# Gate and up weights fetched half a pair ahead, in one ring of eight tiles shared with the down projection

## The chip, the cores and the metric

The kernel runs on one core of a Trainium2 chip. The metric is the device time of one execution in microseconds; the time before is the median of three runs, 2311.24 us (2308.6 to 2313.23). All data are float32, and products are made on TensorE from operands that are split into a high and a low part.

## The reference

One decoder layer over 2048 tokens and 16 meta tokens, model width 1024, feed-forward width 2816. What matters here is the end of the layer:

```python
h = layer_norm(ALPHA * h + mix, ln1_g[l], ln1_b[l])          # mix: attention and gated linear attention, projected
ffn = swiglu(h, w_ffn_gate[l], w_ffn_up[l], w_ffn_down[l])   # silu(h @ w_gate) * (h @ w_up), then @ w_down
h = layer_norm(ALPHA * h + ffn, ln2_g[l], ln2_b[l])
return h[:, N_META:]
```

## The kernel before

The layer runs in stages. Up to about 920 us: input norm, projections, window attention, the chunked gated linear attention, and the output projection, tile by tile. Then gate and up (about 937 to 1858 us), then the down projection (1858 to 2292 us) with the last norm. The end of the output projection overlaps the first products of gate and up, in an order written out by hand (`FIRST_PRODUCTS`).

**Gate and up.** The tokens are in two blocks `tb` of 1024, the feed-forward width in `NP` = 11 pairs `p` of two tiles of 128. For each `(tb, p)` the product of a 2x2 blocked weight with a 2x2 blocked activation is made by a Strassen scheme: seven products instead of eight, in the order b11, t2, t1, b21, t3, t4, b22. `weights(p, tb)` allocates the four weight quarters `a11, a21, a22, a12` (128x1024 float32, 512 KB each) in the ring with the tag `x2` and four tiles, issues their loads on SP (L1307), and then yields, product by product, the split factor: GpSimd makes `s1 = a21 + a22` (L1319), then `a21 = a11 - a21`, `a11 = s1 - a11` and `a12 = a12 - a11` in place (L1315). `parts` copies a quarter rounded (ScalarE, L183) and takes the rest (L184: GpSimd for pa11, ps2, pa12, pa22, VectorE for ps1, ps3, ps4) into one of four tiles `whl`. The trace names the quarters `a`, their factors `pa` and `ps`. TensorE makes 24 matmuls of 128x512 for each product (L195: `b` and `t`), into two banks. VectorE adds products together (L1382: `u`, `c`, `p`), gates them (L1332, L1333: `sa`, `sb`), GpSimd combines the results (L1414 to L1420: `sc`, `s`), and SP stores seven pieces of each pair to DRAM (L1361).

The activation operands `h_b...`, `h_t...` of a block are split once per block (`make`: loads at L670 and L673 into a ring `mk` of three, L183/L184 on ScalarE, VectorE and GpSimd) and stay in SBUF. Those of the second block are made inside the last pair of the first (about 1400 to 1470 us). Their sums are made by `combine` (L632 to L638, `cb`), which the code puts in pairs 2 to 5 of the first block.

**Down projection.** Again seven products, in the order 1, 6, 7, 4, 5, 2, 3 (`MULS`), each over 11 tiles of the contraction in six steps (`GROUPS`: one tile, then five times two). A step of two tiles has 48 matmuls (L1196, `d`). `fetch_step(k)` loads the two activation tiles `rA` (L1166, or L1169) into a ring of four in the pool `dp`, and the weights into the ring `x2` (`quarter_of` at L1110, `kept` at L1116): one tile for products 1, 2, 3 and 5, two for 7 and 4, three for 6. GpSimd subtracts (L1101), product 6 keeps two results in DRAM (`keep`, L1121), and `split_step` makes the factors `A` and `B` (L183 on ScalarE, L184 on VectorE). A step is fetched two steps ahead and split one step ahead. At the end of each product VectorE takes the banks out (`end_product`, L1104 `y`), with residual rows loaded at L1231 and scaled by GpSimd at L1232.

**What sets the order.** The code only gives a program order and the tiles. The build is opened with `schedule_with_timeline_sim=True`: it simulates the program, and puts into each engine's queue, SP's included, what is ready in the simulation, earlier program order first. So a load or an addition can stand in its queue far ahead of its place in the code when its tile is free in the simulation. On the chip every queue runs strictly in that order. Pools opened with `reuse_waits="tile"` lie where closed pools lay, and a new tile there waits for the old ones under it.

Of the kernel before, what the change touches and what calls it, by code (L numbers as in the profile page):

```python
# [8 lines left out]
F32 = mybir.dt.float32  # L9
# [5 lines left out]
P = 128  # L15
D = 1024
# [4 lines left out]
NP = NF // 2  # L21
# [102 lines left out]
def body(ctx, tc, t, seq):  # L124
    nc = tc.nc
# [11 lines left out]
    NTB = seq // TF  # L137
# [44 lines left out]
    def split_into(hi, lo, src, lo_eng=None):  # L182
        nc.scalar.activation(hi, src, AF.Copy)  # L183
        (lo_eng or nc.vector).tensor_tensor(lo, src, r32(hi), op=ALU.subtract)  # L184
# [17 lines left out]
    def staging(name):  # L202
        return wpool.tile([P, D], F32, tag="x", name=name, bufs=3)
# [59 lines left out]
    with ExitStack() as c1:  # L263
# [5 lines left out]
        ps = c1.enter_context(tc.tile_pool(name="ps", bufs=1, space=PSUM))  # L269
# [350 lines left out]
    pools = {}  # L620
# [60 lines left out]
    ps = c1.enter_context(tc.tile_pool(name="gps", bufs=1, space=PSUM, reuse_waits="tile"))  # L681
# [394 lines left out]
    fp = hops.enter_context(tc.tile_pool(name="fp", bufs=1, reuse_waits="tile"))  # L1076
# [6 lines left out]
    def bank(name):  # L1083

        banks[0] += 1
        first = banks[0] <= 2 * len(EARLY) or (banks[0] - 1) % 8 < 4
        pool, tag = (psA, "a") if first else (pools["psB"], "b")
        return pool.tile([P, 512], F32, tag=tag, name=name, bufs=4)
# [11 lines left out]
    def sub(o, x, y):  # L1100
        nc.gpsimd.tensor_tensor(o, x, y, op=ALU.subtract)  # L1101
# [4 lines left out]
    def quarter_of(i, j, g, name):  # L1106

        ps = GROUPS[g]
        x = fp.tile([P, D], F32, tag="x2", name=f"w{i}{j}_{name}", bufs=4)[:, : 512 * len(ps)]
        nc.sync.dma_start(x.rearrange("p (a b) -> p a b", b=512), t["w_d"][i, j][:, ps[0] : ps[-1] + 1, :])  # L1110
        return x

    def kept(x, g, name):
        n = len(GROUPS[g])
        y = fp.tile([P, D], F32, tag="x2", name=f"{x}_{name}", bufs=4)[:, : 512 * n]
        nc.sync.dma_start(y.rearrange("p (a b) -> p a b", b=512), w_sc[x][g][:, :n, :])  # L1116
        return y

# [4 lines left out]
    def weights_of(q, g, name):  # L1123

        w = lambda i, j: quarter_of(i, j, g, name)
        if q == "1":
            return w(0, 0)
        if q == "6":
            w12, w11, w22 = w(0, 1), w(0, 0), w(1, 1)
            sub(w12, w12, w11)  # L1130
            keep("t1", g, w12)
            sub(w22, w22, w12)
            keep("s6", g, w22)
            return w22
        if q == "7":
            w22, w12 = w(1, 1), w(0, 1)
            sub(w22, w22, w12)
            return w22
        if q == "4":
            w21, s6 = w(1, 0), kept("s6", g, name)  # L1140
            sub(w21, w21, s6)
            return w21
        if q == "5":
            return kept("t1", g, name)
        return w(1, 0) if q == "2" else w(1, 1)
# [9 lines left out]
    raw, factors = {}, {}  # L1155

    def fetch_step(k):

        q, tbs, g = STEPS[k]
        nm = f"{q}_{tbs[0]}_{g}"  # L1160
        tile_ = lambda n: pools["dp"].tile([P, D], F32, tag="rA", name=f"rA{nm}_{n}", bufs=4)
        ps, xs = GROUPS[g], []
        if len(tbs) == NTB:
            for p in ps:
                xs.append(tile_(p)[:, : NTB * HT])
                nc.sync.dma_start(xs[-1].rearrange("p (a b) -> p a b", b=HT), a_sc[MULS.index(q)][p])  # L1166
        else:
            xs.append(tile_(ps[0])[:, : len(ps) * HT])
            nc.sync.dma_start(xs[0].rearrange("p (a b) -> p a b", b=HT), a_last[tbs[0]][:, ps[0] : ps[-1] + 1, :])  # L1169
        raw[k] = xs, weights_of(q, g, nm)  # L1170
# [128 lines left out]

    hops2 = ctx.enter_context(ExitStack())  # L1300
    c2 = ctx.enter_context(ExitStack())
    def weights(p, tb):
        nm = f"{tb}_{p}"
        raw = {}
        for a, (i, j) in (("a11", (0, 0)), ("a21", (1, 0)), ("a22", (1, 1)), ("a12", (0, 1))):
            raw[a] = fp.tile([P, D], F32, tag="x2", name=f"{a}_{nm}", bufs=4)
            nc.sync.dma_start(raw[a], t["w_gu"][p, i, j])  # L1307
        a11, a12, a21, a22 = (raw[a] for a in ("a11", "a12", "a21", "a22"))

        def parts(x, name, eng=None):  # L1310
            hl = wpool.tile([P, 2, D], F32R, tag="whl", name=f"{name}_{nm}", bufs=4)
            split_into(hl[:, 0, :], hl[:, 1, :], x, eng or nc.gpsimd)
            return hl

        sub = lambda o, x, y: nc.gpsimd.tensor_tensor(o, x, y, op=ALU.subtract)  # L1315
        s1 = fp.tile([P, D], F32, tag="s1", name=f"s1_{nm}", bufs=1)
        if (tb, p) != (0, 0) or not early:
            yield parts(a11, "pa11")
        nc.gpsimd.tensor_tensor(s1, a21, a22, op=ALU.add)  # L1319
        sub(a21, a11, a21)  # L1320
        sub(a11, s1, a11)
        yield parts(a11, "ps2")
        yield parts(s1, "ps1", nc.vector)
        yield parts(a12, "pa12")
        yield parts(a21, "ps3", nc.vector)
        sub(a12, a12, a11)
        yield parts(a22, "pa22")
        yield parts(a12, "ps4", nc.vector)
# [8 lines left out]
    AFTER, f = {}, None  # L1337
    for what in FIRST_PRODUCTS.split():
        if what[0] == "P":
            f = EARLY[int(what[1])]  # L1340
# [15 lines left out]
    for tb in range(NTB):  # L1356
        for p in range(NP):
            nm = f"{tb}_{p}"
            tl = lambda tag, n: [fp.tile([P, HT], F32, tag=tag, name=f"{n}{w}_{nm}", bufs=2) for w in range(2)]
            w = weights(p, tb)  # L1360
            store = lambda i, x: nc.sync.dma_start(a_last[tb][:, p, :] if i == 6 else a_sc[i][p][:, tb, :], x)  # L1361
            two = lambda x: staging(f"{x}_{nm}")[:, 0 : 2 * HT].rearrange("p (a q) -> p a q", q=HT)
            s4 = fp.tile([P, HT], F32, tag="s4", name=f"s4_{nm}", bufs=1)

            def product(f):
                if (tb, p) == (0, 0) and f in early:
                    banks[0] += 2
                    out = early[f]
                else:
                    hl, out = next(w), []  # L1370
                    for m in range(2):
                        out.append(bank(f"{f}{m}_{nm}"))
                        matmuls(out[m], ffn_terms(hl, ops[f], m))
                if p == NP - 1 and tb + 1 < NTB:
                    ops[f] = make(f, tb + 1)
                if (tb, p) == (0, 0) and f in AFTER:
                    finish_mixing(f)
                return out

            def add(o, x, y):  # L1380
                for i in range(2):
                    nc.vector.tensor_tensor(o[i], x[i], y[i], op=ALU.add)  # L1382

            p1, u2, u4 = tl("p1", "p1"), tl("u2", "u2"), tl("u4", "u4")
            for o, x in zip(p1, product("b11")):
                nc.scalar.activation(o, x, AF.Copy)
            add(u2, p1, product("t2"))
            add(u4, u2, product("t1"))
            add(p1, p1, product("b21"))
            if (tb, p) == (NTB - 1, NP - 1):  # L1390
                hops1.close()
                open_factors()
            sa = two("sa")
            c11 = gate(*p1, sa[:, 0])
            store(0, c11)
            p7 = product("t3")
            add(u2, u2, p7)
            c22 = tl("p1", "c22")
            add(c22, u4, p7)
            sb = two("sb")  # L1400
            c22 = gate(*c22, sb[:, 0])
            store(3, c22)
            add(u2, u2, product("t4"))
            c21 = gate(*u2, sb[:, 1])
            store(5, c21)
            add(u4, u4, product("b22"))
            if tb == 0 and NTB > 1 and 2 <= p < 2 + KT // 2:
                combine(1, p - 2, lambda n: pools["hop1"].tile([P, HT], F32, tag="mk", name=n, bufs=3))
            if (tb, p) == (NTB - 1, NP - 1):
                c2.close()  # L1410
                open_results()
            c12 = gate(*u4, sa[:, 1])
            sc = two("sc")
            nc.gpsimd.tensor_tensor(sc[:, 0], c12, c22, op=ALU.add)  # L1414
            store(4, sc[:, 0])
            nc.gpsimd.tensor_tensor(sc[:, 1], sc[:, 0], c11, op=ALU.subtract)
            store(1, sc[:, 1])
            nc.gpsimd.tensor_tensor(c12, c11, c12, op=ALU.subtract)
            store(2, c12)
            nc.gpsimd.tensor_tensor(s4, c21, sc[:, 1], op=ALU.subtract)  # L1420
            store(6, s4)
# [41 lines left out]
```

## Time and profile before

| | |
|---|---|
| median of 3 runs | 2311.24 us (2308.6 to 2313.23) |
| the profiled execution: its own time | 2313.99 us |
| its span, first to last instruction | 2312.2 us |
| TensorE (PE) busy | 2182.9 us, 94% |
| weight loads of TensorE (PEld) | 1872.3 us |
| VectorE (DVE) | 1583.1 us, 68% |
| GpSimd (POOL) | 1442.7 us, 62% |
| ScalarE (ACT) | 905.6 us, 39% |
| granted clock of TensorE, mean | 0.978 |
| DMA | 378.28 MB, mean 164 GB/s |

Times in the profile are microseconds from the start of the span. L195 is line 195 of the kernel. In the views by window the columns are: the window, its length, busy time and number of instructions of each engine, the granted clock of TensorE as a share of full speed, the mean busy share of the 16 DMA engines, and GB/s. In the views of waits, a row reads: who waited, for whom, the total, how often, the longest. In the timeline, a row is start, duration, engine, line, operation, tiles, count, and in brackets the idle time ahead of it with what ended it. SPq is the instruction queue that issues the loads and stores.

### The profile page before, as it was taken

The numbers are of one execution on the slowest core, as the hardware profiler recorded it, in microseconds if no ns is written. First come the engines' busy times: TensorE is split into PE (matmuls) and PEld (weight loads), VectorE is DVE, ScalarE is ACT, GpSimd is POOL, SyncE is SP. The second block draws the span as 40 slices with busy tenths as digits, with TensorE's granted clock in tenths as the row PEclk, the third lists the DMA queues.
The fourth block names the chain that finished last, engine by engine and source line by source line (L and its number), as shares of the span: only waits on it lengthen the run. The fifth ranks groups of instructions, "written<-read, shape, count | busy, mean of one in ns | idle before, by whom it ended". The sixth has DMA issues, their size and how long they took to land.

```text
span 2312.2 us, 31772 instructions
## 1 busy us (share of the span) xinstructions
PE 2182.9 (94%) x11536; PEld 1872.3 (81%) x11536; DVE 1583.1 (68%) x2443; ACT 905.6 (39%) x1533; POOL 1442.7 (62%) x1049
## 2 busy tenths in 40 slices
PE   6999999999998979898999998999999999999997
PEld 5887888888998979786888887888888888778885
DVE  7787775686868598467766667766676554675676
ACT  5556654545362543452232324323222232222344
POOL 6889875757556383665767677867676653541334
PEclk9999999999999999998999999999999999999998
DMA  8755551435353554746423234423232488565372
GB/s 278 239 156 161 159 191 52 134 129 196 114 197 142 199 189 157 263 169 194 160 79 128 80 126 146 146 96 115 95 128 78 146 317 298 206 224 183 125 248 101
DMA packets 174206, 378.28 MB, mean 164 GB/s; under 512 B 16177, under 2 KB 62162, under 8 KB 174050
## 3 DMA queue, kind: packets, MB, share of 16 engines
q1 hardware_dynamic: 170242, 373.81, 47.6%
q10 hardware_dynamic: 3808, 2.45, 0.3%
q8 instruction: 91, 1.49, 0.3%
q14 instruction: 65, 0.53, 0.1%
HBM read 258.76 MB, written 117.44 MB: 163 GB/s over the span
## 4 chain that ended last, share of the span: by engine, by line
PE 59%; DVE 18%; POOL 8%; DMA 6%; issue 5%; ACT 4%; SPq 0%; POOLq 0%; DVEq 0%; ACTq 0%
PE t L195 13%; PE d L1196 13%; PE b L195 9%; PE pu L195 8%; PE po L195 5%; PE pv L195 3%; DVE xq L974 2%; POOL pa L184 1%; PE oa L561 1%; DVE y L1104 1%; POOL a L1315 1%; PE lp L980 1%; DMA r_t<-t_sc 1%; DVE sb L1332 1%; DVE cb L637 1%
## 5 line engine op out<-in xcount | busy, mean ns | idle before, releaser
L1196 PE MATMUL d<-B,A 128*128 128x512 f32 x1848 | 426.2, 393 | 10.6 <-DVE A L184 10.6
L1196 PEld LDWEIGHTS d<-B,A 128*128 128x128 f32 x1848 | 350.3, 190 | 86.3 <-DVE A L184 13.0
L195 PE MATMUL t<-h_t,ps 128*128 128x512 f32 x1584 | 377.0, 395 | 18.2 <-DVE ps L184 6.1
L195 PEld LDWEIGHTS t<-h_t,ps 128*128 128x128 f32 x1584 | 301.1, 191 | 85.0 <-ACT ps L183 6.8
L195 PE MATMUL pu<-h,hl_u 128*128 128x512 f32 (+1 forms) x1008 | 247.0, 390 | 2.6 <-ACT hl_u L183 1.0
L184 POOL TENSOR_TENSOR pa<-a,pa 128x1024 fp32r<-128x1024 f32 x65 | 174.3, 2681 | 119.5 <-ACT pa L183 119.5
L195 PE MATMUL b<-h_b,pa 128*128 128x512 f32 x1032 | 241.4, 389 | 0.0
L195 PEld LDWEIGHTS b<-h_b,pa 128*128 128x128 f32 x1032 | 193.6, 188 | 40.1
L195 PE MATMUL po<-hl_o,msh 128*128 128x256 f32 x1024 | 203.1, 294 | 6.3 <-POOL hl_o L184 4.0
L195 PEld LDWEIGHTS pu<-h,hl_u 128*128 128x128 f32 x1008 | 180.3, 193 | 33.7 <-ACT hl_u L183 1.2
L184 DVE TENSOR_TENSOR A<-rA,A 128x1024 fp32r<-128x1024 f32 (+1 forms) x78 | 109.9, 1429 | 125.2 <-ACT A L183 125.2
L183 ACT ACTIVATE ps<-a 128x1024 fp32r<-128x1024 f32 x66 | 69.9, 1059 | 263.8 <-POOL a L1315 209.8
L195 PEld LDWEIGHTS po<-hl_o,msh 128*128 128x128 f32 x1024 | 166.8, 197 | 7.8 <-POOL hl_o L184 4.8
L183 ACT ACTIVATE A<-rA 128x1024 fp32r<-128x1024 f32 (+1 forms) x78 | 78.9, 1043 | 239.4 <-PE d L1196 219.9
L195 PE MATMUL po<-hl_o,msl 128*128 128x256 f32 x512 | 149.3, 292 | 0.0
L184 POOL TENSOR_TENSOR hl_u<-st_u,hl_u 128x1024 fp32r<-128x1024 f32 x48 | 117.2, 2444 | 37.4 <-ACT hl_u L183 37.0
L195 PE MATMUL t<-h_t,pa 128*128 128x512 f32 x528 | 123.7, 389 | 1.4 <-POOL h_t L184 1.4
L195 PE MATMUL b<-h_b,ps 128*128 128x512 f32 x528 | 123.6, 389 | 0.0
L974 DVE TENSOR_TENSOR xq<-e,gqk 64x128 f32<-64x128 f32 x224 | 119.1, 532 | 3.1 <-PE lp L980 0.2
L1382 DVE TENSOR_TENSOR u<-u,t 128x512 f32<-128x512 f32 x132 | 89.0, 678 | 44.4 <-PE t L195 44.3
L1332 DVE SCALAR_TENSOR_TENSOR sb<-sb,u 128x512 f32<-128x512 f32 x22 | 49.9, 2268 | 99.3 <-ACT sb L1331 99.2
L195 PEld LDWEIGHTS t<-h_t,pa 128*128 128x128 f32 x528 | 99.0, 188 | 22.3 <-POOL h_t L184 1.7
(319 smaller groups left out, 4742.2 us busy)
## 6 DMA issues: line engine op xcount, KB each, us to landing
a<-w_gu SPq DMA_DIRECT2D x88, 512.0 KB, 4.6
rA<-a_sc SPq DMA_DIRECT2D x66, 512.0 KB, 5.4
st_u<-w_u SPq DMA_DIRECT2D x56, 512.0 KB, 4.1
w<-w_d SPq DMA_DIRECT2D x50, 512.0 KB, 4.8
hT_sc<-h SPq DMA_DIRECT2D x32, 512.0 KB, 4.5
gh<-hT_sc SPq DMA_DIRECT2D x16, 1024.0 KB, 8.6
st_o<-w_o SPq DMA_DIRECT2D x32, 512.0 KB, 4.7
a_sc<-sa SPq DMA_DIRECT2D x44, 256.0 KB, 4.1
```

Of the source, the lines that this page charges most:

```text
L183: nc.scalar.activation(hi, src, AF.Copy)
L184: (lo_eng or nc.vector).tensor_tensor(lo, src, r32(hi), op=ALU.subtract)
L195: nc.tensor.matmul(out, l, r, start=(i == 0), stop=(i == n - 1))
L561: nc.tensor.matmul(oa[:, n], l, m, start=False, stop=(hh == 1 and i == 5))
L637: nc.vector.tensor_tensor(o, x, y, op=how)
L974: nc.vector.tensor_tensor(x[rows[hh], :, hh, :].rearrange("p j (b c) -> p j b c", c=c), eq[rows[hh]], qv[rows[hh], :, :, 1, :], op=ALU.mult)
L980: nc.tensor.matmul(o[:, P * j : P * j + P], kl[:, j, :], x[:, j].rearrange("p h q -> p (h q)"), start=True, stop=True)
L1104: (eng or nc.vector).tensor_tensor(o, x, y, op=ALU.add)
L1196: nc.tensor.matmul(pt, a_[:, a, ca], fb[:, b, cb], start=(p == 0 and j == 0), stop=(p == NP - 1 and j == 2))
L1315: sub = lambda o, x, y: nc.gpsimd.tensor_tensor(o, x, y, op=ALU.subtract)
L1332: nc.vector.scalar_tensor_tensor(tt, tt, 1.0, g, op0=ALU.add, op1=ALU.mult)
L1382: nc.vector.tensor_tensor(o[i], x[i], y[i], op=ALU.add)
```

## The change

The four loads of a pair leave `weights` for a function `fetch_weights`, which the pair before calls after its fourth product (b21); `weights` only fetches for itself where nothing was fetched. The last pair of the first block fetches for the first pair of the second. The ring `x2` has eight tiles in place of four. The activation tiles `rA` of the down projection leave their own ring of four and go into `x2` too, so that the eight are shared there. The descriptor scratch of the build goes from 8192 to 2048 bytes, which is SBUF space (the kernel issues its loads and stores from SP and ScalarE). Up to the down projection the ring takes 16 KB more of each partition, and the pool `hop1` behind it (operands t1 and b21 and the ring `mk`) moves up by as much; from the down projection on the sum is as before.

```diff
     def quarter_of(i, j, g, name):
-        x = fp.tile([P, D], F32, tag="x2", name=f"w{i}{j}_{name}", bufs=4)[:, : 512 * len(ps)]
+        x = fp.tile([P, D], F32, tag="x2", name=f"w{i}{j}_{name}", bufs=8)[:, : 512 * len(ps)]
...
     def kept(x, g, name):
-        y = fp.tile([P, D], F32, tag="x2", name=f"{x}_{name}", bufs=4)[:, : 512 * n]
+        y = fp.tile([P, D], F32, tag="x2", name=f"{x}_{name}", bufs=8)[:, : 512 * n]
...
     def fetch_step(k):
-        tile_ = lambda n: pools["dp"].tile([P, D], F32, tag="rA", name=f"rA{nm}_{n}", bufs=4)
+        tile_ = lambda n: fp.tile([P, D], F32, tag="x2", name=f"rA{nm}_{n}", bufs=8)
...
+    quarters = {}
+
+    def fetch_weights(p, tb):
+
+        raw = quarters[tb, p] = {}
+        for a, (i, j) in (("a11", (0, 0)), ("a21", (1, 0)), ("a22", (1, 1)), ("a12", (0, 1))):
+            raw[a] = fp.tile([P, D], F32, tag="x2", name=f"{a}_{tb}_{p}", bufs=8)
+            nc.sync.dma_start(raw[a], t["w_gu"][p, i, j])
+
     def weights(p, tb):
         nm = f"{tb}_{p}"
-        raw = {}
-        for a, (i, j) in (("a11", (0, 0)), ("a21", (1, 0)), ("a22", (1, 1)), ("a12", (0, 1))):
-            raw[a] = fp.tile([P, D], F32, tag="x2", name=f"{a}_{nm}", bufs=4)
-            nc.sync.dma_start(raw[a], t["w_gu"][p, i, j])
+        if (tb, p) not in quarters:
+            fetch_weights(p, tb)
+        raw = quarters.pop((tb, p))
...
             add(p1, p1, product("b21"))
+            if p + 1 < NP:
+                fetch_weights(p + 1, tb)
+            elif tb + 1 < NTB:
+                fetch_weights(0, tb + 1)
...
-    nc = bacc.Bacc("TRN2", target_bir_lowering=False, num_devices=1, dynamic_dma_scratch_size=8192)
+    nc = bacc.Bacc("TRN2", target_bir_lowering=False, num_devices=1, dynamic_dma_scratch_size=2048)
```

## The prediction, made before the changed kernel was run

> **What bounds the kernel now.** I read the page's busy shares first, then the stages from the output projection to the end by window, then what TensorE waited for in each stage, then the granted clock around those waits, and last who waits for the weight loads that the change moves.
>
> ```profile
> span 2312.2 us, 31772 instructions
> PE 2182.9 (94%) x11536; PEld 1872.3 (81%) x11536; DVE 1583.1 (68%) x2443; ACT 905.6 (39%) x1533; POOL 1442.7 (62%) x1049
> ```
>
> TensorE is the bound over the whole. The windows say that in gate and up it is the bound without remainder (columns: window, length, busy time of PE, PEld, DVE, ACT, POOL with counts, clock, DMA share, GB/s):
>
> ```profile
> 1225.00:1300.00 75.00, 75.00 (x333) 62.12 (x332) 49.73 (x49) 20.96 (x26) 53.59 (x24) 1.00 0.30 104
> 1526.60:1564.70 38.10, 38.10 (x170) 31.56 (x169) 26.00 (x27) 10.81 (x15) 27.34 (x13) 1.00 0.30 104
> 1600.00:1700.00 100.00, 100.00 (x443) 82.84 (x442) 70.86 (x70) 28.57 (x36) 73.16 (x34) 1.00 0.32 113
> ```
>
> No idle time, full clock, 443 matmuls in 100 us, so 225.7 ns for each and 38.1 us for a pair. What is left to win lies outside: TensorE's waits near the start of gate and up (first three rows, from 900 to 1100 us), at the change of block (next two, 1400 to 1490), and in the down projection (last, 1858 to 2312).
>
> ```profile
> PE nt L781 <- ACT yo L180: 7.4, 2, 4.3
> PE t L195 <- DVE ps L184: 6.1, 1, 6.1
> PE t L195 <- DVE c L1382: 3.8, 1, 3.8
> PE t L195 <- ACT ps L183: 4.4, 1, 4.4
> PE t L195 <- POOL ps L184: 3.0, 2, 1.9
> PE d L1196 <- DVE A L184: 10.6, 5, 5.0
> ```
>
> Around these the clock is low as well (PE alone: window, length, busy with count, clock, DMA share, GB/s):
>
> ```profile
> 1075.60:1089.20 13.60, 3.66 (x8) 0.58 0.60 194
> 1089.20:1100.00 10.80, 10.77 (x36) 0.73 0.78 252
> 1433.10:1445.00 11.90, 5.54 (x13) 0.63 0.44 134
> 1995.40:2010.00 14.60, 9.61 (x31) 0.77 0.55 187
> 2064.90:2080.00 15.10, 11.07 (x38) 0.77 0.80 294
> ```
>
> So a stall costs its idle time and slow matmuls behind it. At 225.7 ns the matmuls recorded there are 9.9 us of work in 24.4 us (first two rows: 14.5 lost), 2.9 in 11.9 (9.0 lost), 7.0 in 14.6 (7.6 lost) and 8.6 in 15.1 (6.5 lost): 37.6 us in four places. That is the whole stock that earlier loads could draw on.
>
> The Trainium skill, "TensorE: Matmul & The Clock Gate", section "What's actually happening", says that the array falls to half clock after an idle window of about 3.4 us and needs about as long a busy one to return. The trace agrees in kind (0.58 and 0.73 after a 6.1 us wait). By that rule each of the stalls of 4 to 6 us costs about 1.7 us beyond its idle time, an estimate, where the rows give 4.2 us for the first place with its two stalls and 4.6 for the second; the sum goes by the rows.
>
> **The change part by part.** *Loads of gate and up in the steady pairs.* Same 88 loads, same bytes. What waits for them is GpSimd:
>
> ```profile
> L1307 SPq DMA_DIRECT2D a<-w_gu x88: 328/333/1042, 923.3 to 1803.9; - x88
>   DMA a<-w_gu: 67.7, 19
> a<-w_gu SPq DMA_DIRECT2D x88, 512.0 KB, 4.6
> ```
>
> GpSimd's 67.7 us of waiting (19 times, 3.6 us each) go away, and TensorE gets nothing for them: it has no idle time in those windows, and a pair's 27.3 us of GpSimd and 26.0 of VectorE lie inside its 38.1. If that cover were gone, the loads would be worth those 3.6 us a pair. On SP four issues of 333 ns come ahead of the stores of the pair's first results: 1.3 us, and who reads these stores is the down projection. With eight tiles the issue needs the tiles of the pair before the running one, which are free by then, so it should not block SP. I take 0, for 19 of the 22 pairs.
>
> *The first pairs.* Here the loads are on the path:
>
> ```profile
> 1006.30 1.41 SPq L1307 DMA_DIRECT2D a<-w_gu  x2
> 1053.26 1.58 SPq L1307 DMA_DIRECT2D a<-w_gu  x2
> 1059.00 2.39 POOL L1319 TENSOR_TENSOR s<-a,a 128x1024 f32<-128x1024 f32 x1 [8.79 <-DMA a<-w_gu]
> 1078.35 0.69 DVE L637 TENSOR_TENSOR cb<-cb,cb 128x512 f32<-128x512 f32 x1 [3.06 <-DMA cb<-n_scT]
> 1081.23 1.22 DVE L184 TENSOR_TENSOR ps<-s,ps 128x1024 fp32r<-128x1024 f32 x1
> 1050.00:1100.00 50.00, 39.70 (x156) 31.35 (x155) 38.29 (x44) 10.04 (x13) 27.21 (x14) 0.83 0.63 201
> ```
>
> The third pair's last two quarters are issued at 1053.26, when the second pair's tiles come free; GpSimd starts the sum only at 1059.00 after 8.79 us of nothing, and the chain of factors from there reaches TensorE at 1082, 6.1 us late; VectorE, behind by then, holds the banks for 3.8 more. With eight tiles these loads can take the first pair's tiles, which in the trace go to the second pair's loads at 1006.30. They land some 40 us earlier, and the sum starts when GpSimd is free, up to 8.8 us sooner. Most that can come back: 14.5 by TensorE, but VectorE's 38.29 us of work in this 50 us window allow only 11.7. Least: 0, since the last releaser is VectorE, which in the quoted rows stands behind an addition `cb` that waited 3.06 us for a load that this change does not move. I take 7, near the 8.8 of the wait removed, less something for VectorE, which is late next.
>
> *The change of block.* The loads of the second block's first pair are placed ahead of where they were, among the operand loads.
>
> ```profile
> 1417.07 2.51 POOL L1319 TENSOR_TENSOR s<-a,a 128x1024 f32<-128x1024 f32 x1 [0.83 <-DMA a<-w_gu]
> 1400.00:1450.00 50.00, 43.64 (x178) 35.00 (x177) 34.74 (x33) 19.74 (x30) 40.90 (x23) 0.90 0.57 179
> ```
>
> The sum waited only 0.83 us here, but GpSimd does 40.9 us of work in 50 us, the operand splits among it, and every 2.5 us operation that it could do earlier, in the 3.6 us holes that the steady pairs leave, shortens the queue ahead of the factor that TensorE wants at 1433. Least 0 (GpSimd's work is the limit and its order stays), most 9.0. I take 4, one such hole.
>
> *The descriptor scratch and the moved pool.* SP and ScalarE issue the loads, not GpSimd; 0. The operands t1 and b21 lie 16 KB higher and wait for other old tiles. The nearest wait of that kind is 1.4 us for `h_t`, so 0, give or take 1.4.
>
> *The start.* The second pair's loads are now free to go out as soon as their tiles exist, about 925 to 940 us, since the simulated order fills SP's queue with whatever is ready.
>
> ```profile
> 920.00:945.00 25.00, 15.73 (x82) 12.57 (x80) 18.20 (x26) 17.55 (x24) 17.02 (x10) 0.80 0.95 348
> 945.00:960.00 15.00, 14.65 (x101) 13.62 (x102) 5.54 (x6) 7.41 (x10) 10.22 (x6) 1.00 0.98 338
> ```
>
> There the DMA engines are full: 95% and 98% at 348 and 338 GB/s. Four loads of 512 KB are 2.1 MB, 6.0 us at that rate, and what is queued behind them on SP are the loads of the output projection's weights, for which TensorE waits next. The cost is between 0 (they slip behind 960, where it is quiet) and 6.0 plus a slow clock of 4.2. I take 2: TensorE's own waits here, 7.4 us, are for `yo`, a computed tile, not for a load. The Trainium skill, "DMA: Bandwidth & Descriptors", section "Issuing engines are not separate DMA queues", says that all loads interleave on the same 16 DMA engines, whoever issues them; by that rule the full 6 us are pushed onto something, an estimate that speaks against the change, and the sum would be 10 in place of 14. No row shows yet on what.
>
> *The down projection.* In product 6 the ring of four holds 1.3 steps of three weight tiles, so loads wait for GpSimd's subtractions, GpSimd waits for loads, and the activation tiles queue behind on SP:
>
> ```profile
> 1953.98 2.39 POOL L1101 TENSOR_TENSOR w<-w,w 128x1024 f32<-128x1024 f32 x1 [8.03 <-DMA w<-w_d]
> 1990.36 0.42 SPq L1166 DMA_DIRECT2D rA<-a_sc  x1
> SPq L1110 <- POOL w L1101: 24.4, 10, 2.9
> SPq L1166 <- DVE A L184: 19.6, 14, 6.5
> rA<-a_sc SPq DMA_DIRECT2D x66, 512.0 KB, 5.4
> w<-w_d SPq DMA_DIRECT2D x50, 512.0 KB, 4.8
> L184 DVE TENSOR_TENSOR A<-rA,A 128x1024 fp32r<-128x1024 f32 (+1 forms) x78 | 109.9, 1429 | 125.2 <-ACT A L183 125.2
> L183 ACT ACTIVATE A<-rA 128x1024 fp32r<-128x1024 f32 (+1 forms) x78 | 78.9, 1043 | 239.4 <-PE d L1196 219.9
> ```
>
> The stall at 2000 comes from `rA` issued at 1990.36. With eight shared tiles product 6 needs five a step, 1.6 steps; its weights no longer wait for each other within a step, they follow activation tiles that are split early. So I count on most of the 7.6 us lost at 1995 to 2010. Products 7 and 4 need four a step, two steps, as before: the 6.5 us at 2065 stay. Products 1, 2, 3, 5 have more room than they use. I take 5, between 7.6 + 6.5 = 14.1 and a loss that the slower rival prices.
>
> **Sum.** 0 + 7 + 4 + 0 - 2 + 5 = 14 us from the profiled execution's own 2313.99, which is 2300; that execution lies 2.75 above the median of 2311.24, so I forecast 2297.
>
> **The rivals.** *Everything comes back.* 11.7 at the start, 9.0 at the change of block and 14.1 in the down projection, with no cost at 940: 34.8, or 2276. For it: one cause, late weight loads, touches all three. Against: VectorE and GpSimd stand at the end of each wait, not a load.
>
> *It does nothing that can be measured.* Gate and up is at 100% anyway, and the stalls are of VectorE behind `cb`, of GpSimd's operand splits and of residual rows, which find the same place in the new order: 2311, within 0.2%, 4.6 us, about what this measurement can tell from no change.
>
> *Slower: the shared ring holds up the activation tiles.* In product 6 an `rA` tile can now get a place only after a weight tile of 1.6 steps ago: 4.8 (its load) + 2.4 + 2.4 (two subtractions) + 2.5 (its split, ScalarE and VectorE) + 5.4 (the `rA` load) + 4.9 (two splits) = 22.4 us, against 1.6 steps of 48 matmuls, 17.3 us. That is 5.1 us per 1.6 steps, 3.2 a step, 19 us over six steps, less the 7.6 that are lost there now: 12 more, 2323. It decides from where the two-step lead with which TensorE enters product 6 is used up. For it: `rA` waits 19.6 us in all already. Against: in most cases the place comes from an activation tile or from a tile that is only subtracted, which is free sooner.
>
> **How the numbers follow.** The forecast, some of each stall recovered, 0.50 (its own range 2291 to 2303: give or take 2 at the start, 4 in the first pairs, 4 in the down projection, as independent parts 6). Everything back 0.12. Nothing measurable 0.18; in it lies the dear end of the start's cost, 10.2 us, with none of the gain in the down projection, which comes to 7 + 4 - 10.2, about nothing. The shared ring slower 0.20. So faster 0.62, same 0.18, slower 0.20. The range leaves out a part of the two outer cases: 2281 to 2319.
>
> **What would show it.** Right: no GpSimd wait for `a` between 1100 and 1850; the windows at 1040 to 1100 and 1430 to 1450 at full clock; product 7 starting without the 5 us wait; gate and up at 38.1 us a pair as before. Wrong: PE waits for `hl_o` or `h_t` between 925 and 990 with SP's w_gu issues just ahead (the start costs more); new PE waits for `A` in product 6 with `rA` issued after `w` (the shared ring); the stalls near 1082 and 1437 still there with weights landed 20 us before (VectorE and GpSimd were the cause, not the loads).

## The result: 0.9% slower, and where the time went

The changed kernel takes 2334.87 us (median of 5 runs, 2331.71 to 2337.0) against 2313.23 us (5 runs, 2308.6 to 2313.41) for the kernel before on the same chip: 1.0092 times, 95% interval 1.0078 to 1.0106. The forecast was 2297. Head of the page after:

```profile
span 2333.0 us, 31802 instructions
PE 2186.8 (94%) x11536; PEld 1872.1 (80%) x11536; DVE 1589.6 (68%) x2443; ACT 913.7 (39%) x1533; POOL 1432.2 (61%) x1049
```

TensorE's same 11536 matmuls take 20.8 us more. To find the place I compare the start of four matmuls in both traces: the last `op` (end of the mixing of the last block of tokens), the last `po` (end of the output projection), the first `d` and the last `d` (down projection). The same four stand in every trace below. "Lost" in gate and up is counted in stretches of 25 us from the last `po`: 25 us less the matmuls that start there at 225.7 ns each; only stretches that lose 1 us or more are counted.

| us | up to last `op` | to last `po` | gate and up | down projection | after it |
|---|---|---|---|---|---|
| before | 910.8 | 88.8 | 858.7 | 436.3 | 17.6 |
| after | 916.2 | 95.0 | 861.4 | 443.1 | 17.3 |
| difference | 5.4 | 6.2 | 2.7 | 6.8 | -0.3 |

**The start, 6.2.** SP's queue and TensorE (b_first is the first product of gate and up) in order of time, and the time from issue to landing of `a_first`; first before, then after, there with a window as well:

```profile
923.34 3.04 SPq L1307 DMA_DIRECT2D a<-w_gu  x4
926.89 0.33 SPq L1038 DMA_DIRECT2D a_first<-w_gu  x1
936.75 6.30 PE L195 MATMUL b_first<-h_b,pa_first 128*128 128x512 f32 x24
```

```profile
DMA to landing us min/median/max: 7.3/7.3/7.3
```

```profile
928.75 4.25 SPq L1309 DMA_DIRECT2D a<-w_gu  x6
933.10 0.39 SPq L1038 DMA_DIRECT2D a_first<-w_gu  x1
943.25 2.08 PE L195 MATMUL b_first<-h_b,pa_first 128*128 128x512 f32 x4 [0.92 <-ACT pa_first L183]
945.87 6.92 PE L195 MATMUL b_first<-h_b,pa_first 128*128 128x512 f32 x20 [0.54 <-DVE pa_first L184]
```

```profile
DMA to landing us min/median/max: 9.0/9.0/9.0
```

```profile
945.00:960.00 15.00, 12.63 (x60) 10.09 (x60) 5.07 (x5) 8.14 (x12) 4.08 (x3) 0.82 1.02 378
```

Six weight loads in place of four stand ahead of `a_first`, which lands 9.0 in place of 7.3 us after its issue. TensorE waits twice, 1.5 us together, and runs at 0.82 of its clock behind that; 24 matmuls that took 6.30 us end 9.5 us after their start. By the last of them TensorE is 4.3 us later than before, and 11 us further on by the whole 6.2, with waits of 0.2 to 0.6 us between. The DMA engines are full at 378 GB/s. The Trainium skill, "DMA: Bandwidth & Descriptors", section "Issuing engines are not separate DMA queues", says that loads interleave on the same 16 engines whoever issues them; the 9.0 against 7.3 us agrees, with all of these loads issued on SP.

**Gate and up, 2.7.** The stalls of before are gone from the places where they were, and as much is lost at others: 17.3 us in the first 150 us (8.7 at 25 to 50, 1.1, 6.0 at 100 to 125, 1.5) for 15.1 before (75 to 100), and 11.1 at the change of block (1.5, 5.1, 4.5 at 425 to 500) for 11.6 before. TensorE after, its two large waits; VectorE ahead of the second; and GpSimd's first wait in the window 1040 to 1850:

```profile
1056.11 1.22 PE L195 MATMUL b<-h_b,ps 128*128 128x512 f32 x2 [8.58 <-ACT h_b L183]
1118.12 6.64 PE L195 MATMUL t<-h_t,ps 128*128 128x512 f32 x22 [4.20 <-DVE ps L184]
```

```profile
1114.38 1.49 DVE L637 TENSOR_TENSOR cb<-cb,cb 128x512 f32<-128x512 f32 x1 [3.77 <-DMA cb<-n_scT]
1115.78 2.28 DVE L184 TENSOR_TENSOR ps<-a,ps 128x1024 fp32r<-128x1024 f32 x1
```

```profile
POOL s L1327 <- DVE ps L184: 98.5, 19, 7.4
```

GpSimd no longer waits for weights. It waits the same 19 times for VectorE, which has to finish `ps` before the one tile of the sum `s1` is free again. And `ps` stands in VectorE's queue behind `cb`, which waits 3.77 us for a load.

**The down projection, 6.8.** TensorE's waits in it, the three largest of them, and SP and VectorE around the first two (`y` is a result that VectorE takes out of the banks at the end of a product, `res` the residual rows added to it):

```profile
PE d L1196 <- DVE A L184: 9.2, 3, 5.5
PE d L1196 <- DVE y L1104: 7.2, 3, 4.2
```

```profile
1995.69 2.33 PE L1196 MATMUL d<-B,A 128*128 128x512 f32 x9 [2.40 <-DVE y L1104]
2007.00 74.68 PE L1196 MATMUL d<-B,A 128*128 128x512 f32 x318 [4.17 <-DVE y L1104]
2087.15 124.28 PE L1196 MATMUL d<-B,A 128*128 128x512 f32 x537 [5.46 <-DVE A L184]
1986.76 5.67 SPq L1166 DMA_DIRECT2D rA<-a_sc  x2
1995.06 3.32 SPq L1231 DMA_DIRECT2D res<-n_sc  x3
2002.10 6.27 SPq L1231 DMA_DIRECT2D res<-n_sc  x4
2002.94 3.41 DVE L1104 TENSOR_TENSOR y<-y,res 128x512 f32<-128x512 f32 x2 [2.51 <-POOL res L1232]
```

The waits for `y` are new; the wait of 4.99 us for `A` that stood at 2000 before is gone. SP is held 5.67 us by two `rA` issues; the residual rows behind them go out late, VectorE waits for them, and the ends of product 6 hold TensorE's banks. Who held the `rA` issues (L1166) between 1900 and 2120:

```profile
SPq L1166 <- POOL w L1101: 15.0, 6, 2.6
SPq L1166 <- DVE B L184: 14.0, 11, 3.5
SPq L1166 <- DMA s<-w_scs: 10.4, 4, 4.7
SPq L1166 <- DVE A L184: 8.0, 6, 1.8
```

Before, the same issues waited almost only for activation tiles, 19.6 us in all (1900 to 2110); now for everything that passes through the shared ring.

**The first 911 us, 5.4.** On all five engines the order of instructions up to the last `op` is the same in both traces, and in those of all kernels below. That stretch took from 908.8 to 916.6 us in the twelve. The four kernels with the old ring of four took 908.8 to 914.4 there, the eight others 910.5 to 916.6, so no run shows that the change adds anything to it.

### The profile page after: what moved, and what is told of

It reads as the page before. It is cut to its first block, busy times and chain, and to the rows that moved or that the text cites. A ratio compares the mean times of both kernels' runs of the same rounds, so it can differ in the third digit from the quotient of the medians.

```text
span 2333.0 us, 31802 instructions
## 1 busy us (share of the span) xinstructions
PE 2186.8 (94%) x11536; PEld 1872.1 (80%) x11536; DVE 1589.6 (68%) x2443; ACT 913.7 (39%) x1533; POOL 1432.2 (61%) x1049
## 4 chain that ended last, share of the span: by engine, by line
PE 60%; DVE 16%; DMA 10%; POOL 5%; issue 4%; ACT 4%; SPq 0%; POOLq 0%; DVEq 0%; ACTq 0%
PE t L195 16%; PE b L195 11%; PE d L1196 11%; PE pu L195 6%; PE po L195 5%; PE pv L195 3%; DVE xq L974 2%; DMA w<-w_d 2%; DVE y L1104 1%; DMA cb<-n_scT 1%; PE lp L980 1%; PE oa L561 1%; DMA r_t<-t_sc 1%; POOL w L1101 1%; DVE cb L637 1%
## 5 line engine op out<-in xcount | busy, mean ns | idle before, releaser
L1196 PEld LDWEIGHTS d<-B,A 128*128 128x128 f32 x1848 | 350.1, 190 | 93.2 <-DVE A L184 11.6
L195 PE MATMUL t<-h_t,ps 128*128 128x512 f32 x1584 | 371.7, 392 | 8.4 <-DVE ps L184 6.1
L184 POOL TENSOR_TENSOR pa<-a,pa 128x1024 fp32r<-128x1024 f32 x65 | 169.2, 2606 | 103.8 <-ACT pa L183 103.8
L184 DVE TENSOR_TENSOR A<-rA,A 128x1024 fp32r<-128x1024 f32 (+1 forms) x78 | 118.0, 1537 | 95.9 <-ACT A L183 95.9
L183 ACT ACTIVATE A<-rA 128x1024 fp32r<-128x1024 f32 (+1 forms) x78 | 78.2, 1040 | 154.1 <-PE d L1196 147.9
L1323 POOL TENSOR_TENSOR a<-a,a 128x1024 f32<-128x1024 f32 x44 | 122.6, 2785 | 1.7
L195 PEld LDWEIGHTS b<-h_b,ps 128*128 128x128 f32 x528 | 99.1, 188 | 30.2 <-ACT h_b L183 8.8
L1327 POOL TENSOR_TENSOR s<-a,a 128x1024 f32<-128x1024 f32 x22 | 53.5, 2434 | 106.5 <-DVE ps L184 106.5
```

The lines of the kernel that those rows point to most:

```text
L195: nc.tensor.matmul(out, l, r, start=(i == 0), stop=(i == n - 1))
L1196: nc.tensor.matmul(pt, a_[:, a, ca], fb[:, b, cb], start=(p == 0 and j == 0), stop=(p == NP - 1 and j == 2))
```

## The experiments

Each ratio is against runs of the kernel before on the same chip (medians 2308.47 to 2313.8 us). The four stages given are those of the table: up to the last `op`, the start, gate and up, the down projection.

**Ring of eight without the early call.** Edit, from the changed kernel:

```diff
-            if p + 1 < NP:
-                fetch_weights(p + 1, tb)
-            elif tb + 1 < NTB:
-                fetch_weights(0, tb + 1)
```

> The changed kernel with the ring of eight tiles and its sharing kept, but the four loads of the next pair placed again where the pair begins, as before the change. Theory: the order on SP is made from what is ready, and with eight tiles the loads are ready anyway, so they still go out ahead of a_first near 928 us: about 2335, as the changed kernel, and TensorE's first b_first matmul as late as there (943 us). Rival: the place in the program decides, and without it the start goes back to 2329 and the stalls of before at 1082 and 1437 come back in part: 2313 to 2329.

2331.89 us, ratio 1.0089 (1.0075 to 1.0104); stages 913.8, 94.4, 863.1, 443.0. As the theory said. SP still has

```profile
926.36 3.87 SPq L1309 DMA_DIRECT2D a<-w_gu  x6
930.33 0.39 SPq L1038 DMA_DIRECT2D a_first<-w_gu  x1
```

The number of tiles made the loads early; the call half a pair ahead added nothing that shows in the stages.

**Descriptor scratch alone.** From the kernel before: `dynamic_dma_scratch_size=8192` to `2048`.

> The kernel before with nothing changed but the descriptor scratch, 2048 in place of 8192. Theory: it costs nothing, and the 5.4 us by which the changed kernel is late at 911 us, with the same order of instructions up to there, come from elsewhere: 2311 to 2313, and the last op matmul starts within 2 us of 910.9. Rival: the scratch (and the addresses that move with it) is what makes the first 911 us slower: 2316 to 2319, with the last op matmul near 916.

2313.7 us, 1.0008 (0.9994 to 1.0022); stages 908.8, 89.0, 859.1, 430.8. The scratch costs nothing. Since its instructions are those of before, it also says how far stages of one program differ from run to run: 2.0 us in the first, 5.5 in the down projection.

**Two rings of four.** From the changed kernel:

```diff
-        x = fp.tile([P, D], F32, tag="x2", name=f"w{i}{j}_{name}", bufs=8)
+        x = fp.tile([P, D], F32, tag="x2a", name=f"w{i}{j}_{name}", bufs=4)
...
-        tile_ = lambda n: fp.tile([P, D], F32, tag="x2", name=f"rA{nm}_{n}", bufs=8)
+        tile_ = lambda n: fp.tile([P, D], F32, tag="x2b", name=f"rA{nm}_{n}", bufs=4)
...
-            raw[a] = fp.tile([P, D], F32, tag="x2", name=f"{a}_{tb}_{p}", bufs=8)
+            raw[a] = fp.tile([P, D], F32, tag=("x2a", "x2b")[(tb * NP + p) % 2], name=f"{a}_{tb}_{p}", bufs=4)
```

> The changed kernel with the ring of eight split in two rings of four: pairs of gate and up take turns, the weights of the down projection have one and the activation tiles rA the other, as before the change. Gate and up can fetch as far ahead as in the changed kernel. Theory: the 6.6 us lost in the down projection come from the sharing, rA behind weight tiles: 2328, TensorE no longer waits for y near 2000, and SP's wait of the rA loads for GpSimd's weight tiles (15.0 us in product 6 and 7) is gone. Rival: they come from the later or reordered residual loads, which the ring does not decide: 2333 to 2336 with the y wait still there.

2325.15 us, 1.0059 (1.0041 to 1.0077); stages 916.6, 95.0, 863.5, 434.9. The down projection is back where it was, 8.2 us shorter than after; the start is as after, gate and up 2.1 longer. TensorE's only wait in it, and the largest wait of L1166 left from 1900 to 2120:

```profile
PE d L1196 <- DVE A L184: 9.1, 4, 4.4
SPq L1166 <- DVE A L184: 14.1, 10, 1.9
```

The wait for `y` and those for weights are gone. The sharing cost the down projection its 7 us, more than the 5.5 by which one program differs from run to run: the four traces with shared tiles take 441.8 to 444.8 us there and wait 5.3 to 7.2 us for `y`, the other eight take 430.8 to 436.5 and never wait for it.

**The second pair's loads held at the start.** From the changed kernel:

```diff
+            if behind is not None:
+                nc.vector.tensor_copy(raw[a][:, 0:1], behind[:, 0:1])
             nc.sync.dma_start(raw[a], t["w_gu"][p, i, j])
...
-                fetch_weights(p + 1, tb)
+                fetch_weights(p + 1, tb, u2[0] if (tb, p) == (0, 0) else None)
```

> The changed kernel, with only the second pair's four loads held back: one column of each of their tiles is first written by VectorE from u2 of the first pair (ready near 967 us), so the loads cannot go out near 928. Four small VectorE copies are added. Theory: the 6.1 us lost between 911 and 1011 come from these loads ahead of a_first: b_first starts again 0.1 us behind the nt transposes and takes 6.3 us, the last po matmul is 5 to 6 us earlier than in the changed kernel, 2329 in all. Rival: they push the loads of the output projection's last weights behind themselves instead, and the same time is lost near 970: 2335.

2325.72 us, 1.0059 (1.0046 to 1.0073); stages 913.7, 89.2, 863.2, 444.8.

```profile
926.26 2.48 SPq L1311 DMA_DIRECT2D a<-w_gu  x4
929.82 0.33 SPq L1038 DMA_DIRECT2D a_first<-w_gu  x1
939.67 6.48 PE L195 MATMUL b_first<-h_b,pa_first 128*128 128x512 f32 x24
```

```profile
945.00:960.00 15.00, 13.91 (x90) 12.25 (x88) 5.78 (x5) 9.37 (x13) 11.31 (x6) 1.00 0.87 298
```

The start is back to 89.2 us, b_first runs without a wait in about its old time, the window behind it is at full clock again, and nothing is lost near 970. These four loads cost 6 us: the four traces that have them ahead of `a_first` take 94.4 to 95.0 us for the start, the other eight 88.7 to 89.3. The down projection, with the ring still shared, takes 444.8.

**Both repaired, third pair early.** The two rings; pairs 0 and 1 share one, and the third pair's loads, in the other, are held:

```diff
-            if p + 1 < NP:
+            if p + 1 < NP and (tb > 0 or p > 1):
                 fetch_weights(p + 1, tb)
...
+            if (tb, p) == (0, 0):
+                fetch_weights(2, 0, u2[0])
```

> Two rings of four as in the split run. The first and the second pair share one of them, so the second pair's loads wait for the first pair's tiles as before the change (about 992 to 1006 us); the third pair has the other ring and its four loads are held behind one column written by VectorE from u2 of the first pair (about 1020 us), 20 to 35 us earlier than before the change; from there on pairs take turns and fetch half a pair ahead. The order on SP up to 1009 us and the place of the nt transposes between the products are those of before. Theory: the loads are the first cause of the 15.1 us that the kernel before loses between 75 and 100 us behind the last po matmul, and the changed kernel only lost them again because the nt transposes went back: 6 to 8 of the 15 come back, nothing is lost at the start and in the down projection: 2303 to 2308. Rival: VectorE and the operand loads give the same delay whatever the weights do: 2311 to 2314, with the loss still between 75 and 125 us.

2312.26 us, 1.0010 (0.9998 to 1.0022); stages 915.4, 88.8, 860.4, 435.4. Start and down projection are repaired together, and the rest is the rival's case (2311 to 2314): 15.4 us are lost in the first 150 us (1.3, 1.3, 6.5, 1.8, 4.5) for 15.1 before. The wait for `h_b` is down from 8.58 to 1.67 us, with the `nt` transposes again where they were among the products; the largest wait is now for VectorE:

```profile
1044.46 0.73 PE L195 MATMUL b<-h_b,ps 128*128 128x512 f32 x2 [1.67 <-ACT h_b L183]
1086.23 13.93 PE L195 MATMUL t<-h_t,ps 128*128 128x512 f32 x48 [3.39 <-DVE c L1392]
```

The third pair's loads go out 23 to 35 us earlier than before, counted from the last `po`, and GpSimd starts its sum 29 us behind that matmul in place of 59. So early weights alone were worth nothing there.

**Less work for VectorE at the change of block.** From the changed kernel, for the second block's operands. The kernel leaves out the 14 subtractions that make their low parts on VectorE, 20.9 us in the trace after; a scaled copy on ScalarE stands in their place, so its low parts are not the reference's.

```diff
+            if tb and k % 2:
+                nc.scalar.activation(x[:, 0, k], raw, AF.Copy)
+                nc.scalar.activation(x[:, 1, k], raw, AF.Copy, scale=2.0 ** -13)
+            else:
                 split_into(x[:, 0, k], x[:, 1, k], raw, nc.vector if k % 2 else nc.gpsimd)
```

> The changed kernel with one part of VectorE's work around the change of block taken away: the low parts of the second block's operands that VectorE computes (14 subtractions of 128x512) are replaced by a scaled copy on ScalarE, so those low parts are not the reference's. The changed kernel loses 11.1 us there (1.5, 5.1 and 4.5 in the windows 425, 450 and 475 us behind the last po matmul), as much as the kernel before (10.1 and 1.5), though its weights land earlier. Theory: VectorE's work is the limit (23.0 of 25 us busy in the first of these windows), so with 10 us of it gone the loss falls under 5 us: about 2328 in all. Rival: GpSimd or the operand loads are the limit, and 9 us or more stay lost: 2333 to 2336.

2318.71 us (one run; the 2328 expected lies 9 higher, and the first stage alone is 5.7 shorter than in the trace after); stages 910.5, 94.8, 852.2, 441.8. 1.3 us are lost at the change of block in place of 11.1. The window from 425 us behind the last `po`, the changed kernel and this one (in the third group of numbers, VectorE):

```profile
1436.20:1461.20 25.00, 23.74 (x105) 19.38 (x104) 23.28 (x19) 11.25 (x17) 20.25 (x10) 1.00 0.40 117
```

```profile
1430.30:1455.30 25.00, 25.00 (x111) 20.49 (x110) 14.00 (x14) 16.53 (x28) 23.20 (x12) 1.00 0.54 162
```

These subtractions are what the loss hangs on; GpSimd, which now works 23.20 of 25 us, is not the limit. How they reach TensorE is open. In the trace after, its waits there end with GpSimd more often than with VectorE (1436 to 1512):

```profile
PE b L195 <- POOL pa L184: 3.9, 3, 1.9
PE t L195 <- DVE ps L184: 1.9, 1, 1.9
```

The subtractions also hold the three tiles `mk` through which the operand loads pass, and this kernel sets those free sooner as well; no run separates the two.

**The combinations moved out of the first pairs**, with the fetch ahead (from the run with both repaired) and without any of the change (from the kernel before), the same edit:

```diff
             x = tile_(f"cb{tb}_{k}_{kh}{th}")
+            if behind is not None:
+                nc.vector.tensor_copy(x[:, 0:1], behind[:, 0:1])
...
-            if tb == 0 and NTB > 1 and 2 <= p < 2 + KT // 2:
-                combine(1, p - 2, lambda n: ...)
+            if tb == 0 and NTB > 1 and 4 <= p < 4 + KT // 2:
+                combine(1, p - 4, lambda n: ..., u4[0])
```

> The held run (two rings of four, third pair's weights 20 to 35 us early) with the 16 combinations cb of the second block's operands (VectorE, 0.69 us each, 11 us in all, with 16 loads and 16 stores on SP) moved from 1050 to 1125 us to the pairs five to eight, by holding their loads behind one column from u4 of those pairs. Theory: VectorE is what the early loads run into in the first pairs, because cb stands in its queue and waits for loads there; with cb gone the early weights count, and of the 15.4 us lost between 0 and 150 us behind the last po matmul at most 5 stay: 2300 to 2304. Rival: cb only fills holes of VectorE, and the loss is of the operands h_b and of the factors' chain: 10 us or more stay, 2307 to 2312.

> The kernel before with the same move of the 16 combinations cb and nothing of the change: ring of four, each pair's weights fetched when the pair before sets its tiles free. Theory: the third pair's loads still come late (1041 and 1053 us before the change, some us earlier with cb's loads out of SP's queue), GpSimd waits for them, and half of the 15.1 us stays: 7 to 10 us lost, 2303 to 2306, some 4 us above the held run with the same move. Rival: cb alone was the cause and the early loads are worth nothing: the same time as that run within 2 us, and the loss between 75 and 100 us gone.

With the fetch ahead 2308.87 us, 1.0002 (0.9985 to 1.0019), stages 911.1, 88.7, 853.3, 436.5; without it 2323.25 us, 1.0059 (1.0038 to 1.008), stages 914.4, 89.3, 866.2, 434.1. In the first 150 us the one loses 2.0 and the other nothing: the stall that the forecast put down to late weights was `cb`, with early weights and with late ones. The second expectation is wrong on that; it had half of the stall stay, and 2303 to 2306 in all. The move also takes `cb`'s own loads out of SP's queue, so that the third of the third pair's loads goes out 49.9 in place of 53.5 us behind the last `po` and GpSimd no longer waits for it. That this is not what counted is seen in the trace before, in ScalarE's copy of the sum that GpSimd made late, and in what TensorE waited for:

```profile
1074.55 1.04 ACT L183 ACTIVATE ps<-s 128x1024 fp32r<-128x1024 f32 x1
1075.64 0.73 PE L195 MATMUL t<-h_t,ps 128*128 128x512 f32 x2 [0.37 <-ACT ps L183]
1082.51 2.93 PE L195 MATMUL t<-h_t,ps 128*128 128x512 f32 x6 [6.13 <-DVE ps L184]
```

The late sum reaches TensorE through ScalarE with 0.37 us. VectorE could have taken its part of it from 1075.6 on, and did so at 1081.23, behind `cb`.

But `cb` takes its delay along, and there the two differ: in the pairs five to eight (225 to 375 us) 19.3 us are lost without the fetch ahead (4.9, 1.1, 6.0, 6.0, 1.3), 6.0 with it (2.2 and 3.8), about what the first lies above its 2300 to 2304. VectorE and SP without the fetch ahead, and the TensorE wait behind it:

```profile
1248.12 0.69 DVE L639 TENSOR_TENSOR cb<-cb,cb 128x512 f32<-128x512 f32 x1 [3.38 <-DMA cb<-n_scT]
1248.73 3.36 DVE L184 TENSOR_TENSOR ps<-a,ps 128x1024 fp32r<-128x1024 f32 x1
1252.15 6.87 PE L195 MATMUL t<-h_t,ps 128*128 128x512 f32 x22 [3.93 <-DVE ps L184]
1249.27 3.19 SPq L1309 DMA_DIRECT2D a<-w_gu  x2
```

And with it, the same chain, with half the wait for TensorE at its end:

```profile
1282.49 2.88 DVE L639 TENSOR_TENSOR cb<-cb,cb 128x512 f32<-128x512 f32 x1 [3.48 <-DMA cb<-n_scT]
1286.56 5.28 PE L195 MATMUL t<-h_t,ps 128*128 128x512 f32 x22 [1.94 <-DVE ps L184]
```

**The same, with `cb` on GpSimd.** So that no `cb` addition waits in VectorE's queue (both kernels of the last pair of runs; the one-column copies that hold its loads stay there):

```diff
-            nc.vector.tensor_tensor(o, x, y, op=how)
+            (nc.vector if behind is None else nc.gpsimd).tensor_tensor(o, x, y, op=how)
```

> The held run with the combinations cb moved to pairs five to eight, and there computed by GpSimd in place of VectorE (16 operations of 128x512, 1.3 us each against 0.69), so that VectorE's queue never waits for their loads. TensorE's and ScalarE's orders are those of the run before with VectorE. Theory: what that run lost in these pairs (2.2 and 3.8 us, waits for VectorE's ps behind a cb that waits 3.5 us for its load) goes away, since GpSimd has 11 us of slack a pair and its factors are made ahead from weights that have landed: 0 to 1 us lost there, 2302 to 2305. Rival: GpSimd's queue passes the same delay on to pa and ps: 4 to 8 us lost in these pairs, 2307 to 2312.

> The kernel before with the same two moves of cb (to pairs five to eight, on GpSimd) and nothing of the change. It lost 4.9, 6.0 and 6.0 us in these pairs with cb on VectorE. Theory: with the weights only just in time GpSimd waits for them 3.6 us a pair, has no lead, and cb's 5.2 us and load waits a pair make its factors late: 4 to 10 us lost, 2306 to 2312, more than the held run with the same moves. Rival: the weights' early fetch is worth nothing here either: the same as that run within 2 us.

With the fetch ahead 2304.05 us (2302.48 to 2306.62), 0.9949 (0.9937 to 0.9962): 0.5% faster than the kernel before, and so faster than both. Without it 2318.66 us, 1.0018 (1.0007 to 1.0029). Stages 913.4, 88.9, 846.0, 434.8 against 911.7, 88.9, 862.8, 435.2: all of the difference, 16.8 us, is in gate and up. In the pairs five to eight nothing is lost with the fetch ahead and 12.9 us without (3.6, 3.3, 2.0, 4.0), more than the 4 to 10 expected; at the change of block it is 12.7 against 16.8, and 2.0 against nothing in the first 150 us. The second ends above its 2306 to 2312. The faster kernel's trace, one of those pairs, and GpSimd's largest wait from 1040 to 1850:

```profile
1239.00:1277.00 38.00, 38.00 (x169) 31.49 (x168) 24.66 (x29) 10.91 (x13) 33.58 (x18) 1.00 0.49 163
```

```profile
POOL s L1331 <- DVE ps L184: 85.3, 18, 5.1
```

And without the fetch ahead, GpSimd's waits and a TensorE wait:

```profile
POOL s L1321 <- DMA a<-w_gu: 59.5, 19, 5.0
POOL cb L639 <- DMA cb<-n_scT: 31.1, 4, 7.9
```

```profile
1252.95 6.86 PE L195 MATMUL t<-h_t,pa 128*128 128x512 f32 x22 [1.82 <-POOL pa L184]
```

GpSimd works 33.58 of 38 us in these pairs and TensorE never waits, as long as the weights are there. Without the fetch ahead it waits 59.5 us for weights and 31.1 for `cb`'s loads, and `pa` is late. Within the four pairs (1180 to 1380) the 31.1 are for `cb` and only 6.8 for weights. The fourth load of each pair stands behind a one-column copy on VectorE that waits for an earlier `cb` to be stored, 31.5 us in all, and 16.1 with the fetch ahead, where GpSimd never waits for `cb`. So the gain of 12.9 us in these pairs is shown to come with the fetch ahead; which of the two waits carries it is not.

The Trainium skill, "Perfetto Trace Analysis", section "Optimizing Scalar/DVE Operations", says that VectorE and GpSimd share a read port of the on-chip memory, so moving work from one to the other might not help. Here it took gate and up from 853.3 to 846.0 us. The 16 additions in the two runs with the fetch ahead, first on VectorE, then on GpSimd (ns, least/median/most):

```profile
L639 DVE TENSOR_TENSOR cb<-cb,cb x16: 1659/2772/2934, 1190.4 to 1323.9; 128x512 f32<-128x512 f32 x16
L639 POOL TENSOR_TENSOR cb<-cb,cb x16: 1282/1298/1743, 1192.5 to 1324.6; 128x512 f32<-128x512 f32 x16
```

The 0.69 us that the expectations count for one on VectorE are those of the trace before, where the additions with no GpSimd operation beside them took 0.68 to 0.69; here each of the 16 ran beside one. So two things left the queue that TensorE depends on: the wait for the loads (15.0 us) and 39.7 us of slowed additions. No run separates them.

## Why the prediction was wrong

By its own terms, forecast gain and measured gain: steady pairs 0 and 0; first pairs +7 and -2.2 (15.1 lost before, 17.3 after); change of block +4 and +0.5; scratch 0 and 0; start -2 and -6.2; down projection +5 and -6.8. The sum was +14; these come to -14.7, and the first 911 us add 5.4 that no run puts down to the change. One reading of a row was off without touching the sum: the 4.6 us of slow clock at the second stall leave out one of its two waits, and by the idle time of the window itself (11.9 less 5.54) it is 2.6.

- *First pairs.* The step that failed is the 7 "near the 8.8 of the wait removed". The row of GpSimd's 8.79 us wait for `a` was right and was not what set the end. The next row of that fence, VectorE's `cb` waiting 3.06 us for a load, was. Taking `cb` away from before removed all 15.1 us with the weights still fetched only when the pair before sets its tiles free; bringing the weights early with `cb` in place removed nothing. The prediction quoted this row and named it as the reason for a gain of 0.
- *Change of block.* The step "every 2.5 us operation that it could do earlier", said of GpSimd, took GpSimd for the limit. It was not: with VectorE's 14 subtractions away 9.8 of 11.1 us are back while GpSimd works more.
- *The start.* Traffic, place and size (0 to 10.2) were right. Choosing 2 was wrong: it reasoned from TensorE's waits before, which were for `yo`, and passed over `a_first`, which stood next in SP's queue and had no slack (b_first followed the transposes without a wait). The sentence that goes by the Trainium skill, 6 us pushed onto something, gave the size that was measured, and the something was `a_first`. That the sizes agree is in part luck: only two of the four loads stood ahead of `a_first`, which was 1.7 us longer on its way, and the rest is its later issue and the waits and slow clock behind it.
- *Down projection.* The step "they follow activation tiles that are split early" failed. The rival with the shared ring was right on the mechanism: `rA` held by weight tiles, its L1166 waits for GpSimd 15.0 us. Its price of 12 was too high against 6.8, and its last link differed: TensorE waited not for `A` in product 6 but for `y`, through residual rows queued on SP behind the held `rA`. The wait for `A` at 2000, on which the 5 counted, did go, and the waits for `y` took its place.
- *Steady pairs.* Right for this kernel: no loss there before or after. "If that cover were gone, the loads would be worth those 3.6 us a pair" came true in kind when `cb` was put into such pairs: 12.9 to 19.3 us lost in four of them without the early weights, 0 to 6.0 with them.

Left open: how the subtractions at the change of block reach TensorE, and whether `cb`'s waits or its slowed additions cost more on VectorE. Also why the first 911 us take between 908.8 and 916.6 us with the same instructions. The share of `nt` transposes in the 8.58 us wait was seen with the order put back (1.67 us), not tried by moving them alone.

## What to carry to other kernels

When a stall ends with an engine behind a queue, look for what that queue itself waited for, and take that away first: a prefetch for another input gains nothing until then, and can be worth something afterwards (here 13 to 17 us). More tiles in a ring let a scheduler issue loads at the first moment they are possible, not at the moment you wrote; if that moment is a full stretch of DMA, hold them behind a value of the right age. Tiles of different lifetimes in one ring tie the short to the long, and on an in-order queue everything behind them as well.

## What the runs showed of the hardware

A load of 512 KB took 9.0 us in place of 7.3 with two more of its size ahead of it and a third right behind. 24 matmuls with waits of 1.5 us in two parts among them, and the clock at 0.82 in the 15 us around and behind them, took 9.5 in place of 6.30 us. The first 5439 matmuls of TensorE, the same in the same order, differed by 7.8 us in their time between twelve traces. An addition of 128x512 on VectorE took 0.68 to 0.69 us with no GpSimd operation beside it, and 1.66 to 2.93 in the run where each ran beside one.
